# In-projection of a streaming encoder step: token tiles loaded feature-major from a second host layout, row scales applied later

## The chip, the cores and the metric

The kernel runs on one core of a Trainium2 chip. The metric is the device time of one execution in microseconds (us), the median of several runs. TensorE (PE, with its weight loads PEld), VectorE (DVE), ScalarE (ACT) and GpSimd (POOL) compute; SyncE (SP) only issues transfers (DMAs), and ACT and POOL can issue some too. Each engine works through its own list of instructions in order and waits for the others at semaphores.

## The reference

One step of a one-layer encoder on 1024 prompt tokens and 32 tokens of a running stream, 1024 features each. Only its first stage matters here:

```
def rms_norm(x, g):
    xf = x.astype(jnp.float32)
    y = xf * lax.rsqrt(jnp.mean(xf * xf, axis=-1, keepdims=True) + EPS)
    return (y * g.astype(jnp.float32)).astype(x.dtype)
...
    proj = xn @ w_in
    (gq, gk, gv, gg, gr, hq, hf, hi, hg, mq, mk, mv, mi, mf, mo) = jnp.split(proj, pts, axis=-1)
...
        h, st_new = mixer(rms_norm(x, g_mix_pre[l]), st, lb_all[l], w_in[l], gla_w_gate[l],
...
        x = x + rms_norm(h, g_mix_post[l])
```

So each token row is divided by its root mean square, each feature multiplied by a gain `g_mix_pre`, and the result multiplied by `w_in`. Three families of recurrent heads, an output projection and a gated feed-forward network with a short convolution follow.

## The kernel before

**Tiling.** Tokens go in units of 128 (u = 0 to 7; u = 8 is the stream of 32), and units in three groups g: units 0 to 2, units 3 to 5, and units 6, 7 and 8. A group has up to 384 tokens. For each group `inproj` makes all columns of `w_in`, in two forms. Feature-major products (`feat(t)`, t = 0 to 13 without 9, tiles `pf`, 128 features x 384 tokens) have the weights `wf_t` as the stationary operand. Token-major products (`vg(blk)`, blk = 0 to 7, tiles `pv`, 128 tokens x 256 features, 282 in block 0) have x as the stationary operand and the weights `wt_blk` streaming. Every product is made three times, high part by high part and the two mixed ones (`mm3`, L101 to L103): a number is split into a high part (a cast) and a low part (the difference).

**How x gets there.** `load_x` (L150) loads a unit token-major. `scale_x` (L293) squares it and sums each row on ACT (L306, L316), makes the reciprocal root on POOL (L307 and L308, or `rstd_of`, L221 and L222), and multiplies the row by it and by the gains `gx` (on all partitions, L165) on DVE (L310, L319). `norm_group` (L323) turns each unit by eight TensorE transposes (L330, tiles `xt`) in two halves of four; ACT casts the high part `xh` out of PSUM (L333) and DVE subtracts to make the low part `xl` (L334). xh and xl hold one group at a time.

**Order in a group.** `inproj` first makes block 0 unit by unit. Block 0 also yields 26 gate columns (`tgs`, L460), which are turned (`tg`, L518), copied by three ACT instructions (L519 to L521) and feed two small products `z` (L577, L662). Then come the features t = 8, 6, 7, 3, 2, 0, 4, 5, 1, 10 to 13, then blocks 1 to 7. After block 2 the next group's x is loaded (L724), after block 5 it is scaled (L726). `vg_store` (L427) copies values to a tile `vg` and stores them to `v_d`; from block 4 on it makes gates: a tanh on ACT (`vth`), one or two DVE instructions (L440, L442), a product on POOL (L444) and a store to `g_d` issued by POOL (L445).

**Weights.** `weights` (L337) loads a raw tile; ACT (L107) or DVE (L109) casts the high part, POOL or DVE (L110) subtracts for the low part. In group 0 the low part is also stored (`lf_d`, `lt_d`, L355), and later groups load it from there. Raw tiles have three buffers.

**What sets the order.** The instructions are put into their order on each engine by a scheduler when the program is built, from its own simulated times; `high_priority` and `issue_after` bend it. The recurrent heads of group g (the `mixer`, small TensorE products `sc`, `sm`, `mi`, `og`) are merged into the in-projection of group g + 1. The PSUM pool `psb` has three buffers, which pv, xt, tg, z and pf share: a product begins when what its buffer held before has been read out. In group 0, feat(7) got the buffer of feat(8) before, and feat(3) gets it now. In the first 400 us SP's and ACT's transfers share eight semaphores in turn, so one is issued when the eighth before it has landed.

## Time and profile before

| what | us |
|---|---|
| median of 3 runs | 1355.11 (1354.75 to 1355.43) |
| span of the profiled execution | 1355.3 |
| busy: PE / DVE / ACT / POOL | 1310.8 / 1025.2 / 709.8 / 317.6 |
| first TensorE instruction | 9.68 |
| first product of `feat(8)`, group 0 | 26.28 |
| first product of `feat(3)`, group 0 | 40.85 |
| first product of `feat(8)`, group 1 | 169.08 |

The page gives no time of the profiled execution other than its span, which lies 0.2 us above the median of the runs; the two are used as one here. PE is busy in nearly every slice, so what counts is what keeps it waiting, and when. Matmuls overlap by design: the time from one start to the next is what one costs, not its listed duration.

### The profile page before, as it was taken

How to read it: one execution, taken by the hardware profiler on the slowest of the kernel's cores; microseconds unless marked ns; L12 is line 12 of the kernel's file. 1: busy time of each engine (PE TensorE's matmuls, PEld its weight loads, DVE VectorE, ACT ScalarE, POOL GpSimd, SP SyncE). 2: the span in 40 equal slices, each digit the busy share in tenths (PEclk: the TensorE clock that was granted, in tenths of full speed). 3: DMA queues.
4: the chain of work that ended last, by engine and by line, in shares of the span. 5: the costliest groups of instructions: out<-in, count | busy, mean ns of one | idle time of the engine just before them, and what ended most of it. 6: DMA issues, size and time to landing. Idle time of an engine off the chain costs nothing.

```text
span 1355.3 us, 29229 instructions
## 1 busy us (share of the span) xinstructions
PE 1310.8 (97%) x11472; PEld 1196.7 (88%) x11472; DVE 1025.2 (76%) x1921; ACT 709.8 (52%) x1362; POOL 317.6 (23%) x530
## 2 busy tenths in 40 slices
PE   6999999999999999999999999999999999999997
PEld 5999889998888887767899999999999996678885
DVE  5795649768598678876998888888888876499566
ACT  5555556555574555435654554545554545454552
POOL 4532303135032254213211212111111110010005
PEclk9999999999998989989999999999999999999998
DMA  9799778886879963454315457536455239645435
GB/s 342 241 358 363 265 244 258 278 281 211 292 230 308 336 201 125 142 182 103 128 48 188 134 133 189 134 111 180 120 147 154 82 127 397 254 161 146 141 102 124
DMA packets 126881, 269.72 MB, mean 199 GB/s; under 512 B 24167, under 2 KB 59143, under 8 KB 126663
## 3 DMA queue, kind: packets, MB, share of 16 engines
q1 hardware_dynamic: 113111, 244.78, 53.2%
q0 software_dynamic: 9120, 18.62, 7.3%
q10 hardware_dynamic: 4512, 4.46, 1.0%
q8 instruction: 90, 1.47, 0.5%
q14 instruction: 48, 0.39, 0.1%
HBM read 206.72 MB, written 86.18 MB: 216 GB/s over the span
## 4 chain that ended last, share of the span: by engine, by line
PE 63%; DVE 5%; DMA 3%; ACT 3%; issue 2%; POOL 1%; SPq 0%; DVEq 0%; POOLq 0%; ACTq 0%
PE pux L103 5%; PE pux L102 5%; PE pux L101 5%; PE puw L101 3%; PE puw L103 3%; PE puw L102 3%; PE q L101 3%; PE q L102 3%; PE q L103 3%; PE x L101 2%; PE x L102 2%; PE x L103 2%; PE puz L103 2%; PE puz L101 2%; PE puz L102 2%
## 5 line engine op out<-in xcount | busy, mean ns | idle before, releaser
L1409 DVE SCALAR_TENSOR_TENSOR y<-uu,fconv_sb,y 128x1060 f32<-128x1060 f32 x88 | 116.2, 1320 | 36.8 <-ACT y L1407 36.2
L1345 ACT COPY c<-pux 128x272 f32<-128x272 f32 (+1 forms) x132 | 49.3, 375 | 50.5 <-PE pux L103 49.8
L1407 ACT ACTIVATE y<-uu,fconv_sb 128x1060 f32<-128x1060 f32 x44 | 56.1, 1275 | 8.5 <-POOL uu L1403 7.8
L101 PE MATMUL pv<-wt_0h,xh 128*128 128x256 f32 (+1 forms) x192 | 56.3, 293 | 3.6 <-DVE xl L334 1.6
L103 PE MATMUL zp<-woh,cl 128*128 128x512 f32 (+1 forms) x144 | 57.7, 401 | 1.5 <-DVE cl L1106 1.5
L1406 POOL COPY fhalo<-uu 128x2 f32<-128x2 f32 x44 | 16.6, 376 | 180.7 <-DVE uu L1350 180.6
L101 PE MATMUL zp<-woh,ch 128*128 128x512 f32 (+1 forms) x144 | 57.8, 410 | 0.8 <-ACT ch L1105 0.8
L102 PE MATMUL zp<-wol,ch 128*128 128x512 f32 (+1 forms) x144 | 57.9, 402 | 0.0
L103 PE MATMUL pv<-wt_1h,xl 128*128 128x256 f32 (+1 forms) x192 | 55.1, 287 | 0.0
L103 PE MATMUL pv<-wt_0h,xl 128*128 128x256 f32 (+1 forms) x192 | 55.0, 286 | 0.0
L102 PE MATMUL pv<-wt_0l,xh 128*128 128x256 f32 (+1 forms) x192 | 54.8, 286 | 0.0
L101 PE MATMUL pv<-wt_1h,xh 128*128 128x256 f32 (+1 forms) x192 | 54.7, 285 | 0.0
L102 PE MATMUL pv<-wt_1l,xh 128*128 128x256 f32 (+1 forms) x192 | 54.4, 283 | 0.0
L1585 POOL TENSOR_TENSOR gss<-gss 128x1 f32<-128x1 f32 (+1 forms) x9 | 8.2, 906 | 185.0 <-ACT gjk L1578 185.0
L221 POOL TENSOR_SCALAR hrs<-hss 128x5 f32<-128x5 f32 (+3 forms) x27 | 10.1, 375 | 176.5 <-DVE hss L1015 172.6
L831 DVE COPY_PREDICATED P<-masks_sb,sc 128x352 f32<-128x352 int32 (+3 forms) x53 | 37.9, 715 | 5.9 <-PE sc L744 5.0
L101 PEld LDWEIGHTS pv<-wt_0h,xh 128*128 128x128 f32 x192 | 36.4, 190 | 5.3 <-DVE xl L334 2.1
L1403 POOL COPY uu<-uu 128x2 f32<-128x2 f32 x44 | 28.0, 637 | 38.8 <-DVE uu L1350 37.8
L101 PEld LDWEIGHTS pv<-wt_1h,xh 128*128 128x128 f32 x192 | 36.2, 189 | 0.7 <-issue 0.6
L222 POOL TENSOR_TENSOR hrs<-hrs,mhalf 128x5 f32<-128x5 f32 (+3 forms) x27 | 36.2, 1341 | 2.2
L103 PEld LDWEIGHTS pv<-wt_0h,xl 128*128 128x128 f32 x192 | 36.5, 190 | 0.2
L102 PEld LDWEIGHTS pv<-wt_0l,xh 128*128 128x128 f32 x192 | 36.5, 190 | 0.1
(1743 smaller groups left out, 5321.0 us busy)
## 6 DMA issues: line engine op xcount, KB each, us to landing
wrP<-in_w_dn SPq DMA_DIRECT2D x27, 512.0 KB, 4.4
h_d<-y SPq DMA_DIRECT2D x22, 530.0 KB, 3.7
ht<-h_d SPq DMA_DIRECT2D x22, 530.0 KB, 10.5
wt_0r<-in_w_tok SPq DMA_DIRECT2D x21, 512.0 KB, 5.7
wt_1r<-in_w_tok SPq DMA_DIRECT2D x21, 512.0 KB, 6.3
ws_d<-in_w_dn POOLq DMA_DIRECT2D x20, 512.0 KB, 8.9
wrP<-ws_d SPq DMA_DIRECT2D x20, 512.0 KB, 4.0
wt_0l<-lt_d SPq DMA_DIRECT2D x14, 512.0 KB, 4.5
```

The source lines that it names most:

```text
L101: pe.matmul(ps, lh[0], rh[0], start=first, stop=False, **kw)
L102: pe.matmul(ps, lh[0], rh[1], start=False, stop=False, **kw)
L103: return pe.matmul(ps, lh[1], rh[0], start=False, stop=last, **kw)
L221: pool.tensor_scalar(out, ss, 1.0 / width, eps, op0=ALU.mult, op1=ALU.add)
L222: pool.tensor_tensor(out, out, mhalf[:n, :cols], op=ALU.pow)
L831: dve.copy_predicated(dst, mk.broadcast_to([n, 11, *mk.shape[2:]]), src)
L1345: kept[name] = act.copy(t, ps)
L1403: pool.tensor_copy(u[:, GAP_P:GAP_P + 2], u[:, GAP_S - 2:GAP_S])
L1406: behind["POOL"] = pool.tensor_copy(fhalo[:, j, :], u[:, NCOL - 2:NCOL])
L1407: act.activation(y, u, AF.Identity, scale=fconv[:, j, 2:3], bias=fconv[:, j, 3:4])
L1409: dve.scalar_tensor_tensor(y, uu[i][:, s:s + NCOL], fconv[:, j, s:s + 1], y, op0=ALU.mult, op1=ALU.add)
L1585: pool.tensor_tensor(ss[:n, 0:1], ss[:n, 2:3], ss[:n, 3:4], op=ALU.add)
```

## The change

The host hands over x twice: as before, and as `xpt` and `xst`, feature-major (a partition holds 8 features of one unit, 128 tokens each), with the gains as a small column tile `gmix`. `load_xt` loads a unit feature-major, and the 72 transposes and their PSUM tiles are gone: ACT and DVE split straight from SBUF. The token-major rows are still loaded (`xrow`), now only for the row scales (`row_scale`): a square with row sums on ACT, `rstd_of` on POOL, and a store of the 128 scales to a DRAM row `rs_d`, issued by POOL. `scales_across` then loads the scales of a group as one row on all partitions (`R`), issued by POOL.

In group 0, x is multiplied by the gains alone (two DVE instructions a unit), and the products are scaled where they are read: the 13 `pf` tiles by `R` with one DVE instruction each in PSUM, the pv tiles of blocks 0 to 3 and tgs by a scale factor of ACT's copy, and those of blocks 4 to 7 by one DVE instruction each. In groups 1 and 2, x is multiplied by gain and `R` in one DVE instruction for each of the 8 feature slices of a unit; the rows are loaded by ACT into one buffer, one unit after the other.

```diff
-    x_in = {}
-
-    def load_x(u):
+    xt_in = {}
+
+    def load_xt(u):
         n = 128 if u < 8 else DEC
-        x = p1.tile([128, 1024], F32, tag="x", name=f"x{u}", bufs=3)
-        for c in (slice(0, 512), slice(512, 1024)) if u == 0 else (slice(0, 1024),):
-            sp.dma_start(x[:n, c], xsrc(128 * u, n)[:, c])
+        x = p1.tile([128, 8, 128], F32, tag="x", name=f"xt{u}", bufs=3)
+        for k in (slice(0, 4), slice(4, 8)) if u == 0 else (slice(0, 8),):
+            sp.dma_start(x[:, k, :n], a["xpt"][u][:, k] if u < 8 else a["xst"][:, k])
         return x
 
-    x_in[0] = load_x(0)
...
-    gx = p1.tile([128, 1024], F32, name="gx")
-    act.dma_start(gx, a["grows"][3:4, :].broadcast_to([128, 1024]))
-    wraw = {}
+    gmix = cp.tile([128, 8], F32, name="gmix_sb")
+    act.dma_start(gmix, a["gmix"])
+    xt_in[0] = load_xt(0)
+    wraw, xrow = {}, {}
     for _i, _ks in enumerate(VG0):
         wraw[0, _i] = p1.tile([128, len(_ks), 282], F32, tag="wr", name=f"wt0_0_{_i}r", bufs=3)
         sp.dma_start(wraw[0, _i], a["w_tok0"][:, _ks[0]:_ks[-1] + 1])
-        if not _i:
-            x_in[1] = load_x(1)
-    x_in[2] = load_x(2)
+    for _u in range(3):
+        if _u:
+            xt_in[_u] = load_xt(_u)
+        if _u == 2:
+            break
+        xrow[_u] = mx.tile([128, 1024], F32, tag=("gt", "cat")[_u], name=f"xrow{_u}", bufs=1)
+        sp.dma_start(xrow[_u], a["xp"][128 * _u:128 * _u + 128, :])
+    xrow[2] = pf.tile([128, 1024], F32, tag="fr", name="xrow2")
+    sp.dma_start(xrow[2], a["xp"][256:384, :])
...
+    rs_of, R_of = {}, {}
+
+    def row_scale(u):
+
+        n = 128 if u < 8 else DEC
+        if u < 3:
+            jk = mx.tile([128, 1024], BF16, tag=("k", "b", "qe")[u], name=f"jk{u}", bufs=1)
+        else:
+            jk = mx.tile([128, 1024], BF16, tag="qe", name=f"jk{u}", bufs=1)
+        x = xrow.pop(u)
+        rs = rs_of[u] = p1.tile([128, 1], F32, tag="rs", name=f"rs{u}", bufs=3)
+        ss = p1.tile([128, 1], F32, tag="ss", name=f"ss{u}", bufs=2)
+        act.activation(jk[:n], x[:n], AF.Square, accum_out=ss[:n])
+        rstd_of(rs[:n], ss[:n], n, 1, 1024)
+        pool.dma_start(rs_d[128 * u:128 * u + n], rs[:n])
+
+    def load_row(u):
+        n = 128 if u < 8 else DEC
+        xrow[u] = p1.tile([128, 1024], F32, tag="xrow", name=f"xrow{u}", bufs=1)
+        act.dma_start(xrow[u][:n], xsrc(128 * u, n))
+
+    def scales_across(g):
+        t0, pl, sl = GROUPS[g]
+        R_of[g] = pf.tile([128, pl + sl], F32, tag="th", name=f"R{g}", bufs=1) if g else \
+            mx.tile([128, 384], F32, tag="sq", name="R0", bufs=1)
+        with nc.allow_non_contiguous_dma("a row on all partitions"):
+            pool.dma_start(R_of[g][:, :pl], rs_d[t0:t0 + pl].rearrange("t o -> o t").broadcast_to([128, pl]))
+            if sl:
+                pool.dma_start(R_of[g][:, pl:pl + sl], rs_d[SEQ:SEQ + sl].rearrange("t o -> o t").broadcast_to([128, sl]))
 
     def scale_x(g):
         for (u, off, n) in units_of(g):
-            x = x_in.pop(u, None)
-            x = load_x(u) if x is None else x
+            x = xt_in.pop(u)
             if g == 0:
-                jk = mx.tile([128, 1024], BF16, tag=("gt", "cat", "k")[u], name=f"jk{u}", bufs=1)
-            else:
-                jk = mx.tile([128, 1024], BF16, tag="qe", name=f"jk{u}", bufs=1)
-            rs = p1.tile([128, 1], F32, tag="rs", name=f"rs{u}", bufs=2)
-            if u == 0:
-                ss = p1.tile([128, 2], F32, name="ss0")
-                hs = slice(0, 512), slice(512, 1024)
-                for i, c in enumerate(hs):
-                    act.activation(jk[:, c], x[:, c], AF.Square, scale=1.0 / 32, accum_out=ss[:, i:i + 1])
-                pool.tensor_scalar(rs, ss[:, 0:1], ss[:, 1:2], EPS, op0=ALU.add, op1=ALU.add)
-                pool.tensor_tensor(rs, rs, mhalf[:, :1], op=ALU.pow)
-                for c in hs:
-                    dve.scalar_tensor_tensor(x[:, c], x[:, c], rs, gx[:, c], op0=ALU.mult, op1=ALU.mult)
+                for k in (slice(0, 4), slice(4, 8)):
+                    dve.tensor_tensor(x[:, k], x[:, k], gmix[:, k].unsqueeze(2).broadcast_to([128, 4, 128]), op=ALU.mult)
                 xn_of[u] = x
                 yield
                 continue
-            ss = p1.tile([128, 1], F32, tag="ss", name=f"ss{u}", bufs=2)
-            with tc.issue_after(vgi[0].ins) if vgi else ExitStack():
-                act.activation(jk[:n], x[:n], AF.Square, accum_out=ss[:n])
-            rstd_of(rs[:n], ss[:n], n, 1, 1024)
-            with tc.issue_after(vgi[1].ins) if vgi else ExitStack():
-                dve.scalar_tensor_tensor(x[:n], x[:n], rs[:n], gx[:n], op0=ALU.mult, op1=ALU.mult)
+            with tc.issue_after(vgi[1].ins):
+                for k in range(8):
+                    dve.scalar_tensor_tensor(x[:, k, :n], x[:, k, :n], gmix[:, k:k + 1], R_of[g][:, off:off + n],
+                                             op0=ALU.mult, op1=ALU.mult)
             xn_of[u] = x
             yield
 
@@ -324,14 +346,11 @@
         for (u, off, n) in units_of(g):
             x = xn_of[u]
             for hf in range(2):
-                ps = psb.tile([128, 4, 128], F32, tag="big", name=f"xt{u}{hf}")
-                for k in range(4):
-                    c = 512 * hf + 128 * k
-                    pe.transpose(ps[:, k, :n], x[:n, c:c + 128], ident[:n, :n])
                 s = slice(4 * hf, 4 * hf + 4), slice(off, off + n)
+                k = slice(4 * hf, 4 * hf + 4)
                 with tc.high_priority(offset=AHEAD):
-                    act.copy(xh[(slice(None), *s)], ps[:, :, :n])
-                    dve.tensor_tensor(xl[(slice(None), *s)], ps[:, :, :n], xh[(slice(None), *s)].bitcast(F32), op=ALU.subtract)
+                    act.copy(xh[(slice(None), *s)], x[:, k, :n])
+                    dve.tensor_tensor(xl[(slice(None), *s)], x[:, k, :n], xh[(slice(None), *s)].bitcast(F32), op=ALU.subtract)
             yield
 
...
+            if g == 0:
+                dve.tensor_tensor(ps[:, :T], ps[:, :T], R_of[0], op=ALU.mult)
...
-                vcopies.append(act.copy(o[:n], ps[:n, :256]))
+                vcopies.append(act.copy(o[:n], ps[:n, :256]) if g else
+                               act.activation(o[:n], ps[:n, :256], AF.Copy, scale=rs_of[u][:n]))
...
+            if g == 0:
+                dve.tensor_scalar(ps[:n, :256], ps[:n, :256], rs_of[u][:n], None, op0=ALU.mult)
...
-                    act.copy(tgs[:n, i, :], ps[:n, 256:])
+                    if g:
+                        act.copy(tgs[:n, i, :], ps[:n, 256:])
+                    else:
+                        act.activation(tgs[:n, i, :], ps[:n, 256:], AF.Copy, scale=rs_of[u][:n])
...
+        if g == 0:
+            scales_across(0)
...
-                    x_in[u] = load_x(u)
+                    xt_in[u] = load_xt(u)
+            if blk in (1, 2, 3, 4) and g < 2:
+                us = [u for (u, off, n) in units_of(g + 1)]
+                if blk > 1:
+                    row_scale(us[blk - 2])
+                if blk < 4:
+                    load_row(us[blk - 1])
+                else:
+                    scales_across(g + 1)
...
+            for _u in range(3):
+                row_scale(_u)
```

The scheduler moves more than the diff shows. The names in the rows are the program's, with buffer numbers behind them.

ACT, group 0, from the copy of the second unit's block 0 to the weights' casts; first before, where `wf_8h`, `wf_6h` and `wf_7h` stand among the copies of block 0:

```order
L431 COPY vg_0_236<-pv_0_210 128x256
L211 ACTIVATE lbt<-lbt 128x4
L107 CAST wf_8h<-wf_8r 128x1024
L333 CAST xh_162<-xt_289 128x4x128
L460 COPY tgs_180<-pv_0_260 128x26
L431 COPY vg_0_286<-pv_0_260 128x256
L333 CAST xh_162<-xt_296 128x4x128
L107 CAST wf_6h<-wf_6r 128x1024
L460 COPY tgs_180<-pv_0_303 128x26
L431 COPY vg_0_329<-pv_0_303 128x256
L107 CAST wf_7h<-wf_7r 128x1024
```

and now (`jk3` and `xrow` 1155 belong to units 3 and 4 of group 1):

```order
L311 ACTIVATE jk_1148,ss_1150<-xrow_1042 128x1024
L318 DMA xrow_1155<-in_xp 128x1024
L487 ACTIVATE tgs_196<-pv_0_284,rs_186 128x26
L453 ACTIVATE vg_0_310<-pv_0_284,rs_186 128x256
L548 COPY r_fm_315<-tg_317 16x384
L549 ACTIVATE r_fm_315<-tg_317,rowb_sb 5x384
L550 ACTIVATE r_ig_316<-tg_317,rowb_sb 5x384
L677 ACTIVATE e_378<-e_378 5x384
L107 CAST wf_8h<-wf_8r 128x1024
L107 CAST wf_6h<-wf_6r 128x1024
L607 ACTIVATE fr_377<-z_0_380,vecs_sb 128x384
L107 CAST wf_7h<-wf_7r 128x1024
```

The casts of the feature weights now stand behind all of block 0's copies, behind the tgs path and behind the issue of a row load for group 1. That issue waits for the semaphore that the store of the low weights `wt_0_2l` frees, and the store now stands ahead of the load of `wf_8r` on SP's queue.

DVE, group 0, around the weights' casts (L109) and the first reading of pf; before:

```order
L110 TENSOR_TENSOR wf_6l<-wf_6r,wf_6h 128x1024
L647 SCALAR_TENSOR_TENSOR e_394<-r_fm_332 5x384
L534 SCALAR_TENSOR_TENSOR e_394<-fr_393 128x384
L404 SCALAR_TENSOR_TENSOR y_383<-pc_379,mconv_sb,y_383 128x384 x3
L408 SCALAR_TENSOR_TENSOR y_383<-th_388,y_383 128x384
L534 SCALAR_TENSOR_TENSOR e_394<-fr_393 128x384
L537 TENSOR_SCALAR e_394<-fr_393 128x384
L109 CAST wf_2h<-wf_2r 128x1024
L539 TENSOR_SCALAR e_394<-e_394,lb 128x384
L534 SCALAR_TENSOR_TENSOR e_394<-fr_393 128x384
L537 TENSOR_SCALAR e_394<-fr_393 128x384
L109 CAST wf_0h<-wf_0r 128x1024
```

and now (`R_313` is R of group 0):

```order
L110 TENSOR_TENSOR wf_6l<-wf_6r,wf_6h 128x1024
L563 SCALAR_TENSOR_TENSOR e_378<-fr_377 128x384
L109 CAST wf_2h<-wf_2r 128x1024
L109 CAST wf_0h<-wf_0r 128x1024
L404 TENSOR_TENSOR pf_8_337<-pf_8_337,R_313 128x384
L404 TENSOR_TENSOR pf_6_396<-pf_6_396,R_313 128x384
L404 TENSOR_TENSOR pf_7_435<-pf_7_435,R_313 128x384
L563 SCALAR_TENSOR_TENSOR e_378<-fr_377 128x384
L566 TENSOR_SCALAR e_378<-fr_377 128x384
L425 SCALAR_TENSOR_TENSOR y_367<-pc_363,mconv_sb,y_367 128x384
```

Before, pf of t = 8 went straight to ACT. Now it waits on DVE behind the casts of `wf_2` and `wf_0`, the fifth and sixth feature weights, and then for R.

POOL, end of group 0; before, the scales of units 3 to 5 (`rs`) stand among the gates of blocks 5 and 6:

```order
L444 TENSOR_TENSOR vg_5_1425<-vth_5_1426,gh 128x256
L445 DMA g_d<-vg_5_1425 128x256
L221 TENSOR_SCALAR rs_1463<-ss_1464 128x1
L222 TENSOR_TENSOR rs_1463<-rs_1463,mhalf 128x1
L444 TENSOR_TENSOR vg_5_1456<-vth_5_1457,gh 128x256
L221 TENSOR_SCALAR rs_1470<-ss_1471 128x1
L445 DMA g_d<-vg_5_1456 128x256
L222 TENSOR_TENSOR rs_1470<-rs_1470,mhalf 128x1
L221 TENSOR_SCALAR rs_1477<-ss_1478 128x1
L444 TENSOR_TENSOR vg_6_1522<-vth_6_1523,gh 128x256
L222 TENSOR_TENSOR rs_1477<-rs_1477,mhalf 128x1
L445 DMA g_d<-vg_6_1522 128x256
```

and now (the last unit of block 7 is `vg_7_1733`, unit 5's scale is `rs_1375`, R of group 1 is `R_1381`):

```order
L313 DMA rs_d<-rs_1149 128x1
L228 TENSOR_SCALAR rs_1256<-ss_1257 128x1
L468 TENSOR_TENSOR vg_7_1701<-vth_7_1703,gh 128x256
L229 TENSOR_TENSOR rs_1256<-rs_1256,mhalf 128x1
L469 DMA g_d<-vg_7_1701 128x256
L228 TENSOR_SCALAR rs_1375<-ss_1376 128x1
L313 DMA rs_d<-rs_1256 128x1
L229 TENSOR_TENSOR rs_1375<-rs_1375,mhalf 128x1
L468 TENSOR_TENSOR vg_7_1733<-vth_7_1735,gh 128x256
L313 DMA rs_d<-rs_1375 128x1
L469 DMA g_d<-vg_7_1733 128x256
L325 DMA R_1381<-rs_d 128x384
```

The last scale's store and the load of R now stand behind the last gate of block 7, and the load of R waits for that store. On TensorE the heads' products that stood between the units of block 7 now stand behind it, and most of those that stood behind group 1's feat(8) stand ahead of it.

More of the change, by code (lines that the diff above doesn't have):

```diff
@@ L81 @@
 TC = dict(schedule_with_timeline_sim=True)
-IN_NAMES = ["xp", "xs", "w_feat", "w_tok0", "w_tok", "w_out", "w_up", "w_dn", "vecs", "gcols", "grows", "wg",
+IN_NAMES = ["xp", "xs", "xpt", "xst", "gmix", "w_feat", "w_tok0", "w_tok", "w_out", "w_up", "w_dn", "vecs", "gcols", "grows", "wg",
             "mconv", "mcache", "fconv", "fcache", "s_gh", "s_c", "s_m", "rowb", "masks", "cf"]
@@ L1896, in _layout @@
     gcols = np.asarray(i["g_ffn_pre"])[0].reshape(8, 128).T
-    grows = np.stack([np.asarray(i["g_mix_post"])[0], np.asarray(i["g_ffn_post"])[0], np.asarray(i["g_head"])[0],
-                      np.asarray(i["g_mix_pre"])[0]])
+    grows = np.stack([np.asarray(i["g_mix_post"])[0], np.asarray(i["g_ffn_post"])[0], np.asarray(i["g_head"])[0]])
+    gmix = np.asarray(i["g_mix_pre"])[0].reshape(8, 128).T
+    xpt = np.asarray(i["x_prompt"])[0].reshape(8, 128, 8, 128).transpose(0, 3, 2, 1)
+    xst = np.asarray(i["x_sample"])[0].reshape(DEC, 8, 128).transpose(2, 1, 0)
     wg = np.zeros((128, 192), f)
@@ L1946, in _layout @@
             cf[r0:r0 + dk, 876 + 2 * (t // 3) + (r0 // 32 % 2 if dk == 32 else 0)] = 1.0
-    r = dict(xp=np.asarray(i["x_prompt"])[0], xs=np.asarray(i["x_sample"])[0], w_feat=w_feat, w_tok0=w_tok0, w_tok=w_tok, w_out=w_out,
+    r = dict(xp=np.asarray(i["x_prompt"])[0], xs=np.asarray(i["x_sample"])[0], xpt=xpt, xst=xst, gmix=gmix, w_feat=w_feat, w_tok0=w_tok0, w_tok=w_tok, w_out=w_out,
              w_up=w_up, w_dn=w_dn, vecs=vecs, gcols=gcols, grows=grows, wg=wg, mconv=mconv, mcache=mcache, fconv=fconv,
```

1 line of the change is left out of this document (added).

## The prediction

> **What bounds the kernel now.** First the page, for who is busy:
>
> ```profile
> PE 1310.8 (97%) x11472; PEld 1196.7 (88%) x11472; DVE 1025.2 (76%) x1921; ACT 709.8 (52%) x1362; POOL 317.6 (23%) x530
> PE   6999999999999999999999999999999999999997
> DMA  9799778886879963454315457536455239645435
> ```
>
> TensorE is busy everywhere but in the first slice and the last, so the time is TensorE's work plus what keeps it waiting; whatever delays it early is not made up later. The transfers are fullest in the same early slices that the change touches. The view by stages says how full:
>
> ```profile
> 17.00:36.00 19.00, 18.08 (x123) 15.83 (x122) 7.75 (x20) 11.21 (x22) 6.95 (x7) 1.00 1.01 403
> 40.00:100.00 60.00, 60.00 (x380) 58.88 (x379) 52.22 (x67) 34.35 (x55) 28.26 (x19) 1.00 0.93 315
> 120.00:160.00 40.00, 38.17 (x429) 36.38 (x428) 28.10 (x57) 23.82 (x51) 20.23 (x30) 0.96 0.85 299
> ```
>
> The columns are stage, length, busy time of PE, PEld, DVE, ACT, POOL, granted clock, DMA share, GB/s. From 17 to 36 us the transfers run at their limit, 403 GB/s. From 40 to 100 us TensorE never waits, while DVE is 87% busy. Then the timeline of the start:
>
> ```profile
> 9.68 1.97 PE L330 MATMUL xt<-ident,x 128*128 128x128 f32 x8 [9.68 <-DVE x L310]
> 11.47 1.07 PE L458 MATMUL pv<-wt_0h,xh 128*128 128x282 f32 x3
> 19.27 0.29 PE L102 MATMUL pv<-wt_1l,xh 128*128 128x282 f32 x1
> 19.40 0.60 PE L330 MATMUL xt<-ident,x 128*128 128x128 f32 x4
> 19.76 0.37 PE L103 MATMUL pv<-wt_1h,xl 128*128 128x282 f32 x1
> 20.25 1.05 ACT L107 CAST wf_8h<-wf_8r 128x1024 fp32r<-128x1024 f32 x1 [2.02 <-DMA wf_8r<-in_w_feat]
> 21.38 2.38 POOL L110 TENSOR_TENSOR wf_8l<-wf_8r,wf_8h 128x1024 fp32r<-128x1024 f32 x1 [2.34 <-ACT wf_8h L107]
> 26.28 0.34 PE L101 MATMUL pf<-xh,wf_8h 128*128 128x384 f32 x1
> 40.85 0.34 PE L101 MATMUL pf<-xh,wf_3h 128*128 128x384 f32 x1
> ```
>
> ACT waits for the transfer of wf_8r, which lands at 20.25; both its parts are ready at 23.8, and feat(8) starts at 26.28: 2.5 us of slack behind a full transfer queue.
>
> **The gain.** Four transposes cost TensorE 0.36 us (19.40 to 19.76). Of 18 such sets, six are in each group: 2.2 us a group. In group 0 the first product could also start some 2 us earlier, since it no longer waits for squares, root and transposes. But its next need, wf_8, is a matter of bytes.
>
> **Group 0: bytes, then DVE.** New ahead of wf_0r, the load that DVE's first reading of pf stands behind: xrow of units 0 to 2, 512 KB each, that of unit 4, 512 KB, perhaps that of unit 5, and R, 192 KB. xrow of unit 3 takes the place of gx. That is 2240 to 2752 KB, at 403 GB/s 5.7 to 7.0 us.
>
> ```profile
> 30.81 0.38 SPq L343 DMA_DIRECT2D wf_0r<-in_w_feat  x1
> wf_0r<-in_w_feat SPq DMA_DIRECT2D x1, 512.0 KB, 7.1
> 43.96 0.68 DVE L109 CAST wf_0h<-wf_0r 128x1024 fp32r<-128x1024 f32 x1
> 48.14 0.55 DVE L534 SCALAR_TENSOR_TENSOR e<-fr 128x384 f32<-128x384 f32 x1
> 32.24 0.48 ACT L390 COPY pc<-pf 128x384 f32<-128x384 f32 x1
> ```
>
> Before, wf_0r landed at 30.81 + 7.1 = 37.9; now at 43.6 to 44.9. Then the cast (0.68), the product by R (not in the trace; 384 columns in PSUM, I take L534's 0.55; between 0.4 and 0.7 changes nothing here) and ACT's copy (0.48) that frees the buffer: feat(3) can start at 45.4 to 46.7, taking 0.1 for each of the steps. It stood at 40.85. R itself is no later: POOL issues it behind wf_7l, about 34, and it needs 3 to 6 us.
>
> TensorE alone would be there earlier. wf_8r gets 1729 KB more ahead of it (three xrow, and two stores of low weights, 705 KB, that were behind it, less the gains gh, 512 KB, that were ahead): 4.4 us, landing at 24.7. ACT reaches its cast only behind the tgs path, whose head waits for the store just ahead of wf_8r, landing 1.3 us before it (512 KB):
>
> ```profile
> 30.55 0.47 ACT L519 COPY r_fm<-tg 16x384 f32<-16x384 f32 x1 [2.66 <-PE tg L518]
> 31.04 0.57 ACT L520 ACTIVATE r_fm<-tg,rowb_sb 5x384 f32<-5x384 f32 x1
> 33.35 0.52 ACT L648 ACTIVATE e<-e 5x384 f32<-5x384 f32 x1
> ```
>
> 23.4 + 0.4 (issue) + 0.6 (two copies) + 0.4 (tg) + 0.47 + 2 x 0.57 + 0.6 (DVE's part and waits) + 0.52 = 27.5; wf_8h 28.6, wf_8l 31.0; 22 products at 0.177 us (wf_8h's first to wf_3h's first is three times 24 of them, with tg and z) end at 34.9, two more features at 43.4. So feat(3) starts at the later of 43.4 and 45.4 to 46.7. I take 45.7: **+4.9**, from +2.5 (R's chain hidden) to +6.5.
>
> After that DVE has 13 products by R, 7.2 us, beside 52.2 of 60 us busy: 59.4. It just fits; a reading may be two features late, which the buffers bear. **+0.6**, from 0 to 4. The 12 pv tiles of blocks 4 to 7 cost DVE some 0.35 us each, 4.2 us in a stage where it has 12 free: **+0.4**, 0 to 2.
>
> **Group 1: a chain through DRAM.**
>
> ```profile
> 150.60 0.29 PE L103 MATMUL pv<-wt_1h,xl 128*128 128x256 f32 x1
> 154.44 0.72 POOL L444 TENSOR_TENSOR vg<-vth,gh 128x256 f32<-128x256 f32 x1 [1.14 <-DVE vth L442]
> 155.46 0.58 POOL L445 DMA_DIRECT2D g_d<-vg  x1 [0.30 <-POOL vg L444]
> 169.08 0.34 PE L101 MATMUL pf<-xh,wf_8h 128*128 128x384 f32 x1
> g_d<-vg POOLq DMA_DIRECT2D x12, 128.0 KB, 5.2
> rowb_sb<-in_rowb SPq DMA_DIRECT2D x1, 1.0 KB, 2.4
> ```
>
> Block 7 ends at 150.8, POOL's last gate starts 3.6 us behind it, feat(8) starts 18.3 us behind it. Now, counted from block 7's end: last gate 3.6, 0.7 + 0.3 + 0.6 to the end of the issue of the last scale's store: 5.2; its landing, unknown: 0.5 KB as rowb 2.4, or as g_d 5.2; issue of R 0.6; its landing, again 2.4 to 5.2. R is there at 10.6 to 16.2. I take 2.4 for the small store and 5.2 for R, nearest in size to g_d: 13.4. DVE's own list (19 instructions of some 0.45 us behind the last gate's) would reach the scaling at about 11. Then the work that was spread before stands in a row:
>
> ```profile
> 148.96 0.48 DVE L865 TENSOR_TENSOR Qz<-x,qe 128x128 f32<-128x128 f32 x2
> 153.25 0.69 DVE L334 TENSOR_TENSOR xl<-xt,xh 128x512 fp32r<-128x512 f32 x1
> 139.79 1.06 PE L744 MATMUL sc<-Qz,Ld 64*64 64x32 f32 x60
> 147.29 0.54 PE L744 MATMUL sc<-Qz,k 64*64 64x64 f32 x20
> 174.17 1.06 PE L744 MATMUL sc<-cf_sb,x 128*128 128x11 f32 x8
> 175.16 0.68 PE L744 MATMUL mi<-v,kt 128*32 128x64 f32 x14
> 176.60 1.16 PE L744 MATMUL mi<-v,kt 128*64 128x64 f32 x12
> ```
>
> 24 scalings of 128x128 at about 0.2 us (two take 0.48 from the first's start to the second's end, each overlapping the next a little): 4.8; a low part 0.8 with waits; 66 of the 72 products of block 0 at 0.13 us: 8.6; tg 0.4: feat(8) starts at 28.0, against 18.3. But the heads' products fill part of that wait: 1.9 us that stood inside block 7 (1.06 + 0.54 and a few transposes) and 3.2 that stood behind feat(8) (1.06 + 0.68 + 1.16 and 0.3). 28.0 - 18.3 - 5.1 = **+4.6** with the transposes' gain in it. Bounds: R at 11 gives +2.2, at 16.2 +7.4.
>
> By the Trainium skill's page "DMA: Bandwidth & Descriptors", section "Anatomy of one DMA — SWDGE (gpsimd) path", a DMA issued by GpSimd takes about 2.0 us plus its bytes at 436 GB/s: an estimate of 2.0 for the store and 2.5 for R. g_d's 5.2 in this trace speaks against so short a time in this stage; by the rule the group's term would be 2.2 and the whole 2.4 less.
>
> **Group 2.** Its scales are stored and R loaded while group 1's blocks run, so no chain opens. The transposes go, and with them some waits:
>
> ```profile
> 328.98 0.66 PE L330 MATMUL xt<-ident,x 128*128 128x128 f32 x4 [0.73 <-ACT vth L113]
> 332.75 0.40 PE L101 MATMUL pv<-wt_0h,xh 128*128 128x282 f32 x1 [1.39 <-DVE xl L334]
> ```
>
> **-2.2**, from -3.6 (one of these waits too) to -1. DVE's eight scalings a unit cost 0.3 us more than the one they replace (1.28), among idle time. The rest of the kernel is untouched.
>
> **The sum.** 4.9 + 0.6 + 0.4 + 4.6 - 2.2 = 8.3 us. The profile's span, 1355.3, is 0.2 above the median of the runs; on the runs that gives 1355.1 + 8.3, about **1363.5**. The low ends add up to 0 + 2.5 + 2.2 - 3.6 = +1.1, the high ends to 6.5 + 4 + 2 + 7.4 - 1 = +18.9.
>
> **The rivals.**
>
> Faster. The mechanism is R arriving in time at both places: if wf_0r and R land before feat(7) has ended, and R of group 1 is there when DVE reaches it, the chains vanish, and with wf_8r inside its 2.5 us of slack the full gain is left: 2 us of earlier start and three times 2.2, 1355.1 - 8.6 = 1346.5. It decides at about 2 us later landing of wf_8r; 1.7 MB at 403 GB/s speak against it. Chance 0.10.
>
> About the same. Bytes delay the start by 2.5, R's chains hide all but 2.2 in group 1, and group 2 gives back 2.2: 1357.6. Speaking for it: wf_0r may land sooner than its row says, since the stage's transfers thin out at 36. Chance 0.13.
>
> DVE as the bound of group 0. If DVE's 87% hold no slack, 7.2 us more push TensorE by some 6: 1369.5. Against it: part of DVE's busy time is stretched waiting. Chance 0.12.
>
> A cold clock. The first eight transposes took 1.79 us to the next product (9.68 to 11.47) where two sets of four take 0.72 later: 1.07 us lost behind 9.68 us of idling. Two new idle stretches of over 4 us would lose as much each: 1365.6. Here belongs the Trainium skill's page "TensorE: Matmul & The Clock Gate", section "Part 1: The HAM clock gate", by which an idle window of about 3.4 us halves TensorE's clock until it has been busy as long; the start agrees, and though the granted clock reads 1.00 there, the pace does not. Small products inside the stretches speak against it. Chance 0.05.
>
> The forecast keeps 0.60. That x feature-major loads slower is no rival: a partition's bytes lie together as before.
>
> **How the numbers follow.** About 0.2%, 2.7 us, is what a measurement of this kernel can tell from no change. Faster 0.10; same 0.14, with the forecast's low edge; slower 0.76. The range takes in the same case and reaches to the high ends less what is unlikely to meet: 1355.5 to 1374.
>
> **What would show it.** First product near 9.4; wf_8h cast after 26; TensorE waiting at the start of feat(3) until about 45, on ACT's copy behind DVE's product by R behind the cast of wf_0; a wait of some 8 us in all behind block 7 of group 0, ended by DVE's scaling, itself ended by R's DMA; none at group 2. What would make it wrong: feat(3) before 43, or group 1's R landing under 11 us behind block 7.

## The result, and the profile after

The changed kernel takes **1417.05 us** (median of 6 runs, 1410.04 to 1425.89) against 1355.45 us before (6 runs, 1354.75 to 1358.12): a ratio of 1.046, 95% interval 1.0436 to 1.0483. It is slower, as forecast, but by some 62 us where 8 were forecast and 19 were the high end. Its profiled execution took 1417.07 us, span 1415.3.

The page of the changed kernel: busy times, then TensorE, its granted clock and the transfers in 40 slices of 35 us, then the shares of the chain that ended last.

```profile
PE 1317.2 (93%) x11400; PEld 1200.3 (85%) x11400; DVE 1035.9 (73%) x1990; ACT 712.1 (50%) x1360; POOL 320.6 (23%) x543
PE   3889959987999999999889999999999999999997
PEclk8899959998999999999999999999999999999999
DMA  9879967888778895535523455536554429853435
PE 68%; DVE 12%; DMA 6%; ACT 3%; issue 2%; POOL 1%; SPq 0%; DVEq 0%; POOLq 0%; ACTq 0%
```

TensorE's row has three dents: the start, the slice from 177 us (the turn to group 1) and a shallow one from 319 us (the turn to group 2). Of the chain, 6% is now transfers (3% before). Two of the stages that the prediction read, and two new ones, by the view of windows (length, busy times of PE, PEld, DVE, ACT and POOL, granted clock, DMA share, GB/s):

```profile
17.00:36.00 19.00, 4.92 (x47) 3.85 (x45) 2.25 (x12) 3.58 (x10) 2.72 (x6) 0.69 1.07 141
40.00:100.00 60.00, 55.37 (x280) 50.98 (x281) 39.34 (x51) 27.62 (x41) 31.48 (x17) 0.93 0.79 280
170.00:210.00 40.00, 22.38 (x299) 18.75 (x299) 22.82 (x65) 11.35 (x27) 5.30 (x10) 0.57 0.74 129
300.00:335.00 35.00, 23.42 (x269) 22.61 (x268) 11.26 (x30) 10.71 (x25) 8.65 (x13) 0.80 0.82 160
```

The first row is the one to stop at. From 17 to 36 us, where the transfers ran at 403 GB/s before, the DMA engines are as busy as ever (1.07) and move 141 GB/s, and no compute engine is busy for more than 4.92 of the 19 us. Something holds the DMA engines without moving bytes. The timeline of the changed kernel says from when, and what waits for it:

```profile
13.12 0.79 POOL L313 DMA_DIRECT2D rs_d<-rs  x1 [0.31 <-POOL rs L229]
17.33 0.54 POOL L313 DMA_DIRECT2D rs_d<-rs  x1
19.76 0.54 POOL L313 DMA_DIRECT2D rs_d<-rs  x1
35.29 0.28 ACT L487 ACTIVATE tgs<-pv,rs 128x26 f32<-128x26 f32 x1 [15.36 <-DMA lt_d<-wt_2l]
35.63 0.61 PE L547 MATMUL tg<-ident,tgs 128*16 128x128 f32 x6 [14.08 <-ACT tgs L487]
39.72 0.69 PE L101 MATMUL pf<-xh,wf_8h 128*128 128x384 f32 x1 [3.48 <-ACT wf_8h L107]
```

Three stores of 128 row scales (4 bytes from each partition) are issued at 13 to 20 us. ACT then waits 15.4 us for the store of wt_2l, which was issued at 16.98, just before the second of them; TensorE waits for ACT. At the turn to group 1, the same kernel's timeline of POOL:

```profile
174.21 0.60 POOL L313 DMA_DIRECT2D rs_d<-rs  x1
190.94 0.55 POOL L325 DMA_DIRECT2D R<-rs_d  x1 [15.60 <-DMA rs_d<-rs]
```

And its chain of waits, up to the first of DVE's scalings by R (start, length, what):

```profile
174.21 16.16 DMA rs_d<-rs
190.44 0.51 issue
190.94 5.28 DMA R<-rs_d
196.24 3.25 DVE xt L340 x12
```

The small store takes 16.2 us, R behind it 5.3. Two more such stores had been issued on POOL at 167.67 and 171.56; the second of them took 18.6 us and landed just ahead of this one. At the turn to group 2 the waits sit in POOL's own queue, and DVE and TensorE behind it:

```profile
317.13 0.55 POOL L325 DMA_DIRECT2D R<-rs_d  x1 [15.92 <-DMA rs_d<-rs]
327.01 0.57 POOL L327 DMA_DIRECT2D R<-rs_d  x1 [7.55 <-DMA rs_d<-rs]
327.94 1.36 POOL L229 TENSOR_TENSOR hrs<-hrs,mhalf 128x6 f32<-128x6 f32 x1
329.33 0.56 DVE L1054 TENSOR_TENSOR cat<-og,hrs 128x384 f32<-128x384 f32 x1 [5.18 <-POOL hrs L229]
330.04 1.35 PE L781 MATMUL om<-vm,w 64*64 64x65 f32 x20 [6.24 <-DVE cat L1054]
```

hrs belongs to the mixer of group 1's heads and has nothing to do with R; it only stands behind R's loads on POOL.

### The profile page after: what moved, and what is told of

The parts are those of the page before. It is cut to its first block, busy times and chain, and to the rows that moved or that the text cites. A ratio compares the mean times of both kernels' runs of the same rounds, so it can differ in the third digit from the quotient of the medians.

```text
span 1415.3 us, 29175 instructions
## 1 busy us (share of the span) xinstructions
PE 1317.2 (93%) x11400; PEld 1200.3 (85%) x11400; DVE 1035.9 (73%) x1990; ACT 712.1 (50%) x1360; POOL 320.6 (23%) x543
## 4 chain that ended last, share of the span: by engine, by line
PE 68%; DVE 12%; DMA 6%; ACT 3%; issue 2%; POOL 1%; SPq 0%; DVEq 0%; POOLq 0%; ACTq 0%
PE pux L102 4%; PE pux L103 4%; PE pux L101 4%; PE pv L101 4%; PE pv L103 3%; PE pv L102 3%; PE puw L101 3%; PE puw L103 3%; PE puw L102 3%; DMA rs_d<-rs 3%; PE q L101 3%; PE q L102 3%; PE q L103 3%; PE x L101 2%; PE x L102 2%
## 5 line engine op out<-in xcount | busy, mean ns | idle before, releaser
L101 PEld LDWEIGHTS pv<-wt_0h,xh 128*128 128x128 f32 x192 | 38.1, 198 | 17.2 <-ACT xh L352 10.1
L1052 DVE TENSOR_REDUCE hss<-sq 128x5 f32<-128x320 f32 (+3 forms) x27 | 13.6, 502 | 37.2 <-ACT sq L1051 37.2
L781 PE MATMUL sc<-Qz,Ld 64*64 64x32 f32 (+5 forms) x1344 | 29.4, 223 | 11.9 <-issue 4.3
L781 PEld LDWEIGHTS sc<-Qz,Ld 64*64 64x64 f32 (+2 forms) x1344 | 24.9, 135 | 17.7 <-issue 12.0
```

The source lines that it names most:

```text
L101: pe.matmul(ps, lh[0], rh[0], start=first, stop=False, **kw)
L781: line[0] = fn(*args, **kw)
L1052: dve.tensor_reduce(ss[:n, h0:h0 + nh], sq3, axis=mybir.AxisListType.X, op=ALU.add)
```

## The experiments

Two theories. **Slow stores**: a store of 4 bytes from each of 128 partitions to neighbouring addresses is slow in itself, and holds up the other transfers meanwhile. **Bytes and order**: the second copy of x and the places in the queues make the start late, and a round trip through DRAM is long whatever it carries. Where each run lost time against the kernel before, in us, from the first product of each step in the profiled timelines (before: 26.28, 40.85, 85.47, 169.08, 240.83, 410.01, and 1344.88 for the last product of all). One profile stands for each run; e3's is the slowest of its four executions (1374.84 us), e8's the fastest of its four (1358.45):

| late at | changed | e2 | e5 | e1 | e3 | e6 | e10 | e8 |
|---|---|---|---|---|---|---|---|---|
| feat(8), group 0 | 13.4 | 12.5 | 1.6 | 1.1 | -0.2 | 13.0 | -0.4 | 1.0 |
| feat(3), group 0 | 17.2 | 14.6 | 3.7 | 3.2 | 2.1 | 24.2 | 1.7 | 0.9 |
| block 1, group 0 | 22.5 | 20.1 | 9.2 | 7.5 | 5.7 | 29.0 | 2.3 | 1.9 |
| feat(8), group 1 | 46.4 | 18.7 | 8.3 | 6.2 | 11.2 | 28.1 | 1.8 | 2.2 |
| block 1, group 1 | 42.0 | 32.0 | 10.4 | 8.6 | 9.5 | 26.8 | 1.5 | -0.9 |
| block 1, group 2 | 58.7 | 39.2 | 10.5 | 7.0 | 9.5 | 34.1 | 1.2 | -1.4 |
| last product | 59.5 | 42.7 | 17.2 | 13.8 | 17.6 | 38.7 | 9.7 | 1.6 |

**e1, no stores.**

```diff
-        pool.dma_start(rs_d[128 * u:128 * u + n], rs[:n])
...
-            pool.dma_start(R_of[g][:, :pl], rs_d[t0:t0 + pl].rearrange("t o -> o t").broadcast_to([128, pl]))
+            pool.dma_start(R_of[g][:, :pl], a["grows"][0:1, :pl].broadcast_to([128, pl]))
```

> The changed kernel without the nine stores of rs to rs_d; R is loaded from a row of an input of the same shape, so the products of all groups carry wrong scales. Theory S (each store of one 4-byte value from each of 128 partitions takes about 16 us and holds up the other transfers meanwhile): most of the 62 us go, 1355 to 1372 us. Theory B (the second copy of x and the order of the queues delay the start, and the round trip of R is long whatever it carries): the bytes and the loads of R are still there, 1400 us or more.

Measured: 1371.48 us (one run), just inside the first expectation. 45.6 of the 62 us are gone with nine transfers of at most 512 bytes each; all the bytes of x are still loaded twice. "Bytes and order" is out as the main cause.

**e2, stores that nobody reads.** Only the load of R is changed, as in e1.

> The changed kernel with its nine stores, but R is loaded from a row of an input, so no load has to wait for a store's data; the products carry wrong scales. If the stores cost only by the wait store, then R: the 16 us before R in groups 1 and 2 go and the start too is mended, 1360 to 1375 us. If they hold up the other transfers, the start keeps its 20 us and R still queues behind them: 1390 to 1415 us.

Measured: 1400.24 us (one run). No instruction waits for a scale's store, and yet 28.8 us of e1's gain are lost again: feat(8) is 12.5 us late, as in the changed kernel. So the larger part of the cost is what the stores do to other transfers; waiting for them (the changed kernel against e2) is 16.8 us. Between these three programs the scheduler also moves instructions, so the split is a difference of times and not exact.

**e5, the same stores, 64 bytes apart.**

```diff
-    rs_d = dr.tile([NTOK, 1], F32, name="rs_d")
+    rs_d = dr.tile([NTOK, 16], F32, name="rs_d")
...
-        pool.dma_start(rs_d[128 * u:128 * u + n], rs[:n])
+        pool.dma_start(rs_d[128 * u:128 * u + n, 0:1], rs[:n])
```

> As the run with unread stores (1400 us), but each row scale is stored 64 bytes from the next instead of 4; R still comes from a row of an input, so the products carry wrong scales. If what is slow is many small writes to the same few hundred bytes: 1366 to 1378 us, about that of the run without stores (1371 us). If every 4-byte write is slow wherever it goes: 1390 to 1405 us.

Measured: 1374.82 us (one run). Equal bytes, equal count of writes, equal queue; only the addresses differ, and in the traces DVE, ACT, POOL and SyncE run the same instructions in the same order as in e2. 25.4 of the 28.8 us are back. From issue to landing (smallest, median, largest of the nine), by the view of the tile rs_d in e2:

```profile
DMA to landing us min/median/max: 7.0/11.0/14.4
```

The same in e5:

```profile
DMA to landing us min/median/max: 2.0/4.8/6.5
```

And the windows from 18 to 30 us, e2's, then e5's:

```profile
18.00:22.00 4.00, 4.00 (x35) 3.62 (x34) 2.26 (x12) 2.86 (x8) 2.89 (x6) 1.00 1.20 183
22.00:26.00 4.00, 0.86 (x11) 0.41 (x9) 0.00 (x0) 0.00 (x0) 0.00 (x0) 1.00 0.75 132
26.00:30.00 4.00, 0.00 (x0) 0.00 (x0) 0.00 (x0) 0.00 (x0) 0.00 (x0) 0.74 1.30 126
```

```profile
18.00:22.00 4.00, 4.00 (x35) 3.62 (x33) 2.00 (x12) 2.60 (x7) 2.63 (x6) 1.00 0.95 329
22.00:26.00 4.00, 1.00 (x15) 0.27 (x13) 0.36 (x1) 2.14 (x5) 0.54 (x1) 1.00 0.95 262
26.00:30.00 4.00, 2.14 (x4) 1.00 (x4) 0.89 (x2) 1.69 (x3) 2.10 (x1) 0.65 1.02 376
```

The last column is what the reader is to compare: 183, 132, 126 GB/s with the scales side by side, 329, 262, 376 with them 64 bytes apart.

**e4 and e7, the store by itself.** Stores to scratch in the kernel before, in the up-projection, where transfers have room.

```diff
+        d = dr.tile([n, row], F32, name="prb%d_d" % f)
+        with tc.issue_after(behind["POOL"].ins):
+            eng.dma_start(d[:, :w], ident[:n, :w])
```

> The kernel before with six stores of the identity's columns to scratch that nobody reads, spread over the up-projection, where TensorE is always busy: 128 partitions x 4 bytes side by side from GpSimd's queue (prb6) and from SyncE's (prb9), 4 bytes each 64 bytes apart (prb12) and 512 bytes apart (prb15), 32 partitions x 4 bytes side by side (prb18), 512 bytes each (prb21). Theory S: prb6 and prb9 land after about 16 us, prb18 after about 8, prb21 after 2 to 5; if it is the neighbouring addresses, prb12 or prb15 land after 2 to 5, if it is the 4 bytes, after 16. Rival (only GpSimd's queue is slow): prb9 lands after 2 to 5 and prb21 as late as prb6. The time stays within 2 us of the kernel before.

> The kernel before with eight stores to scratch, spread over the up-projection: 4 bytes from each of 128 partitions, 8, 16 and 32 bytes apart and side by side, from GpSimd's queue, then side by side and 64 bytes apart from SyncE's; and 16 and 64 bytes from each partition, side by side. The first probes landed after 11.4 us side by side and 5.4 us 64 or 512 bytes apart. If writes into one 64-byte piece wait for one another, the landing falls with the distance, from 11 us side by side towards 5 at 32 bytes apart, 64 bytes from each partition land in under 5 and 16 bytes in between; SyncE's side by side lands after 8 or more and transfers beside it drop under 100 GB/s. If only partial writes count, all but the one of 64 bytes land as late as that side by side.

| from each of 128 partitions, GpSimd's queue | landing, us |
|---|---|
| 4 bytes, side by side | 11.4 (e4), 11.8 (e7) |
| 4 bytes, 8, 16, 32, 64, 512 bytes apart | 7.2, 6.5, 5.4, 5.4, 5.5 |
| 16, 64, 512 bytes, side by side | 7.6, 4.5, 3.0 |
| 4 bytes, 32 partitions only, side by side | 8.0 |

What the other transfers did meanwhile, in e4: behind the store side by side (issued at 804.6 us), then behind that with 64 bytes between (928.1):

```profile
804.00:808.00 4.00, 4.00 (x34) 4.00 (x33) 2.44 (x6) 2.74 (x4) 2.23 (x5) 1.00 0.81 251
808.00:812.00 4.00, 4.00 (x35) 4.00 (x34) 3.06 (x4) 1.25 (x3) 0.24 (x2) 1.00 1.48 58
812.00:816.00 4.00, 4.00 (x35) 4.00 (x35) 3.69 (x8) 1.55 (x5) 0.32 (x2) 1.00 0.60 26
...
928.00:932.00 4.00, 4.00 (x34) 4.00 (x33) 1.82 (x4) 1.56 (x3) 2.99 (x6) 1.00 0.91 258
932.00:936.00 4.00, 4.00 (x35) 4.00 (x33) 2.51 (x4) 2.10 (x3) 0.18 (x1) 1.00 0.93 219
936.00:940.00 4.00, 4.00 (x36) 4.00 (x35) 4.00 (x10) 2.11 (x5) 0.70 (x2) 1.00 0.86 204
```

Behind 512 bytes written in 4-byte pieces the DMA engines are busy for 1.48 and 0.60 of their time and move 58 and 26 GB/s; the kernel before, at the same point of the up-projection (798 to 806 us), moves 145 and 77 with shares of 0.64 and 0.19. What the landing falls with, in one store of each kind, is the distance between the pieces, up to 32 bytes. Two things went otherwise than expected. In e4, SyncE's store was issued at 13.5 us, in the middle of the start, and not in the up-projection; it landed after 10.0 us, feat(8) of that kernel started at 33.19 (6.9 late), and the kernel took 1366.91 us (one run), 11.6 more than before where at most 2 were expected. Its window from 18 to 22 us, where the kernel before moves 403 GB/s at a share of 1.01:

```profile
18.00:22.00 4.00, 3.58 (x29) 3.34 (x27) 1.61 (x6) 0.07 (x1) 0.80 (x1) 1.00 0.85 59
```

So a single such store from SyncE's queue stalls the start as well: it is not GpSimd's queue. In e7 no landing is shown for SyncE's two stores, and behind the one side by side the transfers kept 197 and 222 GB/s for 8 us before they fell to 103 (at a share of 1.39): there the effect comes later and is weaker than expected, and in that kernel GpSimd's store side by side left 111 and 101. e7 took 1351.61 us (one run), not slower than before: in the up-projection, where TensorE does not wait for these transfers, the stall cost nothing.

**e6, nine buffers.** In the changed kernel the scales of group 1 share three buffers with those of group 0, which DVE still reads in block 7.

```diff
-        rs = rs_of[u] = p1.tile([128, 1], F32, tag="rs", name=f"rs{u}", bufs=3)
+        rs = rs_of[u] = p1.tile([128, 1], F32, tag="rs", name=f"rs{u}", bufs=9)
```

> The changed kernel with nine buffers for rs in place of three and nothing else: the stores and the loads of R stay, but the scales of group 1 no longer wait for the last scaling by rs in block 7 of group 0. If the 26 us at the turn to group 1 come from where the store stands (behind block 7), they shrink to under 8 and the time to 1385 to 1402 us, the start being as late as in the changed kernel; if the stores' stall reaches TensorE wherever they stand, 1405 us or more.

Measured: 1396.34 us (one run), 20.7 less. Between block 1 of group 0 and feat(8) of group 1 the changed kernel loses 23.9 us, e6 gains 0.9. So this wait came from the place of the stores, and the place from the three buffers. The start is no better, and even 7 us worse at feat(3), where TensorE waits 8.25 us for the reading of pf; the last part comes back to this wait.

**e3, R from TensorE.** No store, no load, and nine buffers for rs as in e6.

```diff
+        ps = psb.tile([128, 512], F32, tag="big", name=f"rp{g}")
+        for (u, off, n) in units_of(g):
+            pe.matmul(ps[:, off:off + n], rs_of[u][:n].broadcast_to([n, 128]), ident[:n, :n], start=True, stop=True)
+        dve.tensor_copy(R_of[g], ps[:, :pl + sl])
```

> The changed kernel with no stores and no loads of R: three products of 128x128 per group (rs repeated along the columns, times the identity) put R on all partitions in PSUM, and DVE copies it; nine buffers for rs instead of three, so that the scales of the next group need not wait for block 7 of this one. Theory S: 1345 to 1362 us, with no wait of TensorE over 3 us at the turn to groups 1 and 2. Theory B: the start keeps its 20 us, 1370 us or more.

Measured: 1371.9 us (4 runs, 1369.21 to 1374.84), ratio to before 1.0118 (1.010 to 1.0136). The waits at the two turns are gone (none over 2 us at either), but it does not reach the 1362 us expected. Its time alone lies where the other theory put it, at 1370 us or more; its start does not (feat(3) is 2.1 us late, not some 20). With the stores out of the way the change still costs 16 us. The next runs look for these.

**e10, e3 without the scaling of group 0's products.**

```diff
-            if g == 0:
-                dve.tensor_tensor(ps[:, :T], ps[:, :T], R_of[0], op=ALU.mult)
...
-            if g == 0:
-                dve.tensor_scalar(ps[:n, :256], ps[:n, :256], rs_of[u][:n], None, op0=ALU.mult)
```

> The run with R from TensorE (1372 us) without VectorE's 13 products by R and 12 scalings by rs in group 0, which leaves out that group's row scale in features and in blocks 4 to 7. If VectorE bounds group 0 (the rival of the prediction at 6 us), 1362 to 1367 us; if its 13 us lie beside other work, 1369 to 1374 us.

Measured: 1366.91 us (4 runs, 1365.77 to 1370.33), 5.0 less than e3 and just inside the first expectation. The 95% intervals of the two ratios, 1.010 to 1.0136 and 1.0062 to 1.0117, overlap, so the size is uncertain; in the profiles the two runs part by 3.4 us up to block 1 and by 9.4 up to feat(8) of group 1. From 40 to 100 us DVE is busy 52.88 us of 60 in e3, as in the kernel before, with TensorE at 55.22 in place of 60 (e3's windows):

```profile
40.00:100.00 60.00, 55.22 (x314) 52.52 (x313) 52.88 (x72) 31.36 (x51) 27.03 (x20) 0.97 0.83 281
```

DVE's work did not grow within the stage; the stage's work took longer, and TensorE lost 4.8 us of it.

**e8, e12, e9, the change in groups 1 and 2 only.** Group 0 is that of the kernel before, R comes from TensorE; in e9 GpSimd multiplies x by the gains beforehand. e12 is e8 once more, for a second profile. The diff below leads from e8 to e9.

```diff
-                    for k in range(8):
-                        dve.scalar_tensor_tensor(x[:, k, :n], x[:, k, :n], gmix[:, k:k + 1], R_of[g][:, off:off + n],
-                                                 op0=ALU.mult, op1=ALU.mult)
+                    dve.tensor_tensor(x[:, :, :n], x[:, :, :n], R_of[g][:, off:off + n].unsqueeze(1).broadcast_to([128, 8, n]),
+                                      op=ALU.mult)
...
+                    pool.tensor_tensor(xt_in[u][:, :, :n], xt_in[u][:, :, :n], gmix.unsqueeze(2).broadcast_to([128, 8, n]),
+                                       op=ALU.mult)
```

> Group 0 as in the kernel before (token-major x, scaled, transposed); groups 1 and 2 take x feature-major, with R made by TensorE and no store of the scales. If TensorE's work bounds the turns to groups 1 and 2, 48 transposes less (4.4 us) and six small products more give 1350 to 1353 us. If what is saved there is lost to the next wait for VectorE, whose scalings of x grow from 3.8 to about 8 us a group, 1354 to 1362 us.

> As the run with groups 1 and 2 only (1363 us), but GpSimd multiplies x by the gains when it is loaded, so that VectorE is left with one product by R per 128 tokens (about 1.3 us, as in the kernel before) in place of eight (2.7 us). If VectorE's extra 4 us a group ate the gain: 1348 to 1355 us. If the turns were not bound by TensorE's transposes at all, or GpSimd's 2.5 us pieces delay the gates of the blocks: 1356 to 1366 us.

> The run with groups 1 and 2 only once more, for a second profile: its times were 1358 to 1365 us, and the profiled execution, the fastest of them, was 1.4 us ahead of the kernel before at block 1 of group 2 and 1.6 us late at the end. If the in-projection itself loses the time in the slower executions, this one is 3 us late or more at block 1 of group 2; if it is lost later, it is ahead there again and loses 4 us or more from there to the end.

Measured: e8 1363.08 us, ratio 1.0078 (1.0049 to 1.0108); e12 1362.25, 1.0057 (1.0031 to 1.0082); e9 1362.79, 1.0055 (1.0034 to 1.0075). So 48 transposes less go with 6 to 10 us more, and VectorE's extra scalings are not the reason, since e9 does without them (GpSimd has the gains there). Inside the in-projection part of the gain is seen: from block 1 of group 0 to block 1 of group 2, e8 gains 3.3 us, e12 1.5 and e9 0.4, where two groups were to give 4.4. But 1.8 to 2.2 us are lost ahead of that stretch, and behind it e8 loses 2.9, e9 3.5 and e12 8.9. Executions of one program differ by as much: e8's four go from 1358.45 us, at a mean granted clock of 0.989, to 1365.14 at 0.984, and the kernel before, beside e11, from 1350.22 at 0.993 to 1364.07 at 0.981. The profiles of e8 (0.989) and e12 (0.981) are two such executions of the same program, so a few us in one profile can't be put down to the change. e8 is above both of its expectations, e9 within its second, and e12's profile speaks in the main for the second of its own: at block 1 of group 2 it is not ahead but 0.7 us late, and it loses far more than 4 us from there on.

**e11, the transposes twice**, in groups 1 and 2 of the kernel before.

```diff
-                    pe.transpose(ps[:, k, :n], x[:n, c:c + 128], ident[:n, :n])
+                    for _ in range(2 if g else 1):
+                        pe.transpose(ps[:, k, :n], x[:n, c:c + 128], ident[:n, :n])
```

> The kernel before with each transpose of x in groups 1 and 2 done twice (48 more, 0.36 us for four: 4.3 us of TensorE's work). If TensorE's work bounds these places, 1359 to 1361 us, and taking the transposes away should have given as much back; if TensorE has to wait for VectorE there anyway, 1354 to 1358 us, and taking them away could give nothing.

Measured: 1365.44 us (median of 9 runs, 1363.06 to 1371.88 and one of 1430.96), ratio 1.0078 (1.0049 to 1.0106): 9 us, twice the work added. In its profile, group 1's 2.2 us vanish (0.2 late at block 1 of group 1), group 2 costs 3.3, and 2.4 more are lost behind the in-projection. Taking the transposes away and doubling them both cost 6 to 10 us: what a few us of TensorE's work here are worth is not read from their own time. Every variant's instruction order differs in the later stages too, which are laid out by a simulated schedule; which of these shifts costs the time stays open.

No version tried beats the kernel before.

## Why the prediction was wrong, step by step

**The step that failed** is the price of the small store: "its landing, unknown: 0.5 KB as rowb 2.4, or as g_d 5.2 ... I take 2.4 for the small store". It was priced by bytes, from rows of transfers that load a few bytes or store whole rows. Measured: 16.2 us at the turn to group 1, 7.8 for the unit of 32 tokens. A second cost was not in the sum at all: while such a store runs, the others crawl. Together the stores are worth 45 us (changed kernel against e1, or e3), of which 28.8 fall on other transfers (e2 against e1) and 16.8 on waiting.

**Group 0's start**, forecast +4.9 at feat(3), came as +17.2, of which 13.4 are there at feat(8). The path named for TensorE was right (ACT's tgs path waits for the store just ahead of wf_8r), but that store was to land at 23.4 and ACT was released at 35.3. The other path, on which the +4.9 rests (DVE's reading of pf behind the cast of wf_0), does end the wait of feat(3) in the changed kernel, as named, but TensorE is so late itself that it waits only 0.56 us:

```profile
56.09 0.91 DVE L109 CAST wf_0h<-wf_0r 128x1024 fp32r<-128x1024 f32 x1 [2.18 <-DMA wf_0r<-in_w_feat]
57.51 0.48 ACT L411 COPY pc<-pf 128x384 f32<-128x384 f32 x1 [7.92 <-DVE pf L404]
58.04 0.45 PE L101 MATMUL pf<-xh,wf_3h 128*128 128x384 f32 x1 [0.56 <-ACT pc L411]
```

In e6 the same path holds it for 8.25 us, since the load of wf_2r, whose cast stands ahead of wf_0's, comes late (DVE waits 17.1 us for it):

```profile
65.02 0.69 PE L101 MATMUL pf<-xh,wf_3h 128*128 128x384 f32 x1 [8.25 <-ACT pc L411]
```

In e1, e2, e3 and e5 the scheduler puts the first product by R ahead of both casts and TensorE does not wait there, so no run tests the +4.9 without the stores. (With 0.1 for each of its three steps that sum gives 45.6 to 46.9, not 45.4 to 46.7; the 45.7 taken lies in both.) The 2.1 us by which feat(3) is late in e3 are clock. In e3, TensorE works 1.9 us of 24 to 28 us, and then:

```profile
28.00:32.00 4.00, 3.78 (x12) 3.47 (x12) 2.75 (x3) 3.06 (x4) 0.83 (x2) 0.50 1.03 418
```

12 products in 4 us at a granted clock of 0.50; at 0.99 a stretch of 4 us holds 24, as two windows of the changed kernel show:

```profile
44.00:48.00 4.00, 4.00 (x14) 4.00 (x14) 0.00 (x0) 1.31 (x3) 2.82 (x2) 0.50 0.99 368
48.00:52.00 4.00, 4.00 (x24) 4.00 (x23) 0.00 (x0) 1.05 (x1) 2.33 (x1) 0.99 1.00 350
```

The rival of the cold clock had a chance of 0.05 and is part of the truth: in the changed kernel the clock is 0.50 from 24 to 48 us, and feat(8) to feat(3) takes 18.3 us in place of 14.6. By the Trainium skill's page "TensorE: Matmul & The Clock Gate", section "Part 1: The HAM clock gate", an idle window of about 3.4 us halves the clock, and it takes at least one busy window of that length to bring it back. The trace of the changed kernel agrees roughly on the fall, 2.7 us after TensorE's last product (21.5 to 24.2), and with "at least": the clock is back only 8.3 us after feat(8) starts.

**DVE's load**, forecast +0.6 and +0.4, is about 5.0 (e3 against e10, with the reserve on its size above). That is the rival "DVE as the bound", sized at 6. Busy 87% was read as 13% of room, and that room was not free where TensorE needed it.

**Group 1**, forecast +4.6, came as +23.9 up to feat(8). Its parts up to R were near but for the store: the last store's issue ended 4.8 us behind block 7 (5.2 forecast), R took 5.3 (5.2), the first 12 scalings 3.25 (24 were to take 4.8); R was there 26 us behind block 7 in place of 13.4. From R to feat(8) it took 19.3 us in place of 14.6, again at a low clock: 0.57 from 170 to 210 us, and block 0's products stand 0.23 us apart in the chain until 208, not 0.13.

**Group 2**, forecast -2.2 since "no chain opens", came as +16.7. POOL waits in order: 15.9 and 7.6 us for the stores, with hrs of the mixer behind. What is queued behind a waiting instruction was counted for group 1, not here.

**The transposes' gain**, -2.2 a group, is in no time measured (e8, e9, e12), and in the profiles 0.4 to 3.3 us of 4.4 are seen inside the in-projection; why is open.

**The rest of the kernel**, untouched by the sum, was not untouched: from block 1 of group 2 to the last product the lateness grows by 6.7 to 8.5 us in e1, e3, e5 and e10 (by 0.8 in the changed kernel). In e3 most of it is lost ahead of the up-projection, whose first `pux` product is 16.9 us late. Why is open.

The sign and the mechanism of a chain through DRAM were right. With the stores out, the change costs 16 us (e3), at the upper end of the range, but not by the terms of the sum; that agreement is luck.

## What to carry to other kernels

A column of 128 single values isn't written to DRAM side by side: give the values to the other partitions by a product on TensorE (three of 128x128 a group here), or write each apart from the next (32 bytes were enough for a single store in e7; 64 were tried in the kernel, in e5, where nobody reads them back). Price a transfer by its pieces and their addresses, not by its bytes, and count what it does to the transfers beside it. When a stage shows a high DMA share and few GB/s, look for the smallest store issued just before, not for the largest.

## What was not expected of the hardware

A store of 512 bytes in 128 pieces of 4 lands after 11.4 to 11.8 us in the up-projection and after 11.2 to 18.6 in the changed kernel's in-projection, 32 pieces after 8.0; 64 bytes apart, 5.4. Meanwhile all 16 DMA engines together move 58 and 26 GB/s in the worst 8 us of e4's first store, and in the changed kernel 56 from 18 to 22 us, where its 76 packets on SyncE's queue and 6 on GpSimd's take 142% of the engines' time:

```profile
q1 hardware_dynamic: 76, 0.20, 114.0%
q0 software_dynamic: 6, 0.02, 28.0%
```

That is 64 us x 1.14 / 76 = 0.96 us for a packet of some 2.6 KB on SyncE's queue; the kernel before moves 468 packets, 1.61 MB, in the same 4 us. The Trainium skill's page "DMA: Bandwidth & Descriptors", section "Specifications", says that below 512 bytes a transfer does a read-modify-write. That fits the small pieces being slow (4.5 us for 64 bytes a partition, 3.0 for 512), but not that 4-byte pieces 32 bytes apart land in half the time of those side by side: the measurement adds the distance. That pieces in one short stretch of DRAM wait for one another is a reading that fits the order of the rows; it is not shown, since the trace does not show the DRAM itself and each row is one store among other traffic.
